# Per-head roots as one power on GpSimd, and rotary products, sums of squares and norm remainders on VectorE

## The chip, the cores and the metric

The kernel runs on one core of one Trainium2 chip. The metric is the device time of one execution in microseconds; the median of three runs of the kernel before is 3424.99 us (3420.28 to 3428.63). TensorE does the matrix products, VectorE and GpSimd elementwise work, ScalarE activations and copies, and SyncE (SP) issues the DMAs. Each engine works through its own instructions in order; semaphores make one wait for another.

## The reference

The reference computes two layers over 1024 latent tokens and 256 context tokens of width 1024. Each layer normalises the tokens (RMS), scales and shifts them by a modulation vector, projects them once, and hands the columns of that projection to latent attention (six heads), a state space part (S5) and windowed attention (six query heads, two key heads). An output projection and a gated feed-forward follow. The change lies in the preparation of queries and keys:

```python
def rms_norm(x, g):
    xf = x.astype(F32)
    y = xf * lax.rsqrt(jnp.mean(xf * xf, axis=-1, keepdims=True) + NORM_EPS)
    return (y * g.astype(F32)).astype(x.dtype)

def mla_queries(c_q, g_lora, w_uq, g_qk, rope):
    q = (rms_norm(c_q, g_lora) @ w_uq).reshape(b, t, MLA_HEADS, MLA_QK)
    q = rms_norm(q, g_qk)
    if rope is not None:
        q = jnp.concatenate([q[..., :MLA_NOPE], apply_rope(q[..., MLA_NOPE:], rope)], axis=-1)

def swa_queries(q_raw, g_qk, rope):
    q = rms_norm(q_raw.reshape(b, t, SWA_HEADS, SWA_HEAD_DIM), g_qk)
    return apply_rope(q, rope) if rope is not None else q
```

So each head of each token needs one reciprocal root of a mean of squares, and its (partial) rotation. Root and rotation commute, because the root is one factor for the whole head.

## The kernel before, in words

Tokens are taken 128 at a time on the partitions. The chunks are 512, 512 and 256 tokens (the last is the context). Every 32-bit product is made of three matmuls of rounded parts: `hi` (rounded on ScalarE) and `lo` (the remainder, made on VectorE), `mm3`. TensorE thus needs both parts of each operand.

The input projection of a layer (lines 522 to 840) works in four kinds of steps, each on a pair of token tiles, 256 tokens. `s1_pair` makes windowed keys and values and the shared rotary part of the latent keys, five pairs. `lora` makes 512-token feature chunks of `c_kv` or `c_q` (`chi`, `clo`, and the squares `csq`, summed over features). `s3` makes latent keys and values from `c_kv`, five pairs; `s5q` latent queries from `c_q`; `s7` windowed queries. The last two have five pairs in layer 0 and four in layer 1, where the context needs no queries. In each step TensorE fills PSUM tiles `tk` (four buffers). ScalarE copies them out to `kb`, `qb` or `sqb` (one tag, three buffers) and squares them into `sq`. VectorE sums the squares (`ssq_of`), takes the reciprocal root (`rsqrt`, eleven instructions), and multiplies by it (`mulr`). GpSimd rotates (`rope`, four products and sums; for context tokens one product with the gain). DMAs on SP write the result to DRAM (`kd`, `qd`, `sqd`, `skd`), from where attention reads it.

`norm_stats` sums the squares of the residual stream and `norm_apply` normalises and splits it. GpSimd takes some of their instructions: the sums for k = 3 and 5, and, with `eng=G`, the remainders for odd k, which need an extra copy on ScalarE. `norm_stats` already takes its root as one power on GpSimd (`rsqrt_pool`, line 180; `rn` in the trace).

The order of the work on each engine is set when the program is built: the source gives priorities, and instructions whose inputs come late let others pass, so that pieces of neighbouring steps are mixed. At run time an engine does not leave that order. Attention follows, mixed with the S5 part, whose tables GpSimd computes in long series.

The lines that the steps of the prediction touch: 170 (`rsqrt`), 273 and 297 (the norms), 568 and 579 (`rope_table`, `rope`), 602 (`rinv`), 620 (`s1_pair`), 643 (`lora`), 668, 705 and 732 (`s3`, `s5q`, `s7`). Many instructions carry the line of a helper, so the tile names tell them apart: L80 is `tt`, L93 and L95 are `ts`, L98 is `stt`, L77 `act`, L65 `mm`.

Of the kernel before, what the change touches and what calls it, by code (L numbers as in the profile page):

```python
# [8 lines left out]
F32 = mybir.dt.float32  # L9
# [23 lines left out]
def trunk(ctx, tc, x, c, ctxt, c_ctx, w_mod, b_mod, norm1, w_in, q_lora_g, w_uq, kv_lora_g, w_ukv,  # L33
# [24 lines left out]
    mhalf = const.tile([128, 4], F32, name="mhalf")  # L58
# [45 lines left out]
    def load_split(hi, lo, raw, srcs, scale=None):  # L104
        """DRAM pieces into raw, then hi = the rounded value and lo = what is left of it."""
        for dst, src in srcs:
            nc.sync.dma_start(out=dst, in_=src)
        if scale is None:
            act(hi, raw)
            sub(lo, raw, f32(hi))  # L110
        else:
            act(hi, raw, AF.Copy, scale=scale)
            stt(lo, raw, scale, f32(hi), ALU.mult, ALU.subtract)

    class Wsets:
        """Rotating sets of (rounded, rest, raw) weight tiles over the pools that are open."""
# [31 lines left out]
    class Side:  # L148
        """A generator of pieces of work, run up to a share of its steps."""
# [20 lines left out]
    def rsqrt(pl, dst, v, shape, tag):  # L170
        i = pl.tile(shape, I32, tag=tag + "i", name="rsi")
        w = pl.tile(shape, F32, tag=tag + "w", name="rsw")
        ts(i, v.bitcast(I32), 1, op0=ALU.logical_shift_right)
        ts(dst.bitcast(I32), i, -1, 0x5F3759DF)
        for _ in range(3):
            stt(w, v, -0.5, dst, ALU.mult, ALU.mult)
            mul(w, w, dst)
            stt(dst, w, 1.5, dst, ALU.add, ALU.mult)

    def rsqrt_pool(dst, v, n):  # L180
        """v to the power of -1/2, in one instruction of the general engine."""
        tt(dst, v, mhalf[:, 0:n], ALU.pow, G)
# [58 lines left out]
    def mod_cols(psf, pl, acc, l, nm, k0, n, nj):  # L241
        """Sums over the partitions of acc, n blocks of 128 columns for each of nj."""
# [13 lines left out]
    def mod_gen(l, nm, nj, pl, psf, w):  # L256
        """One modulation vector, with the sums over the rows on the vector engine."""
# [15 lines left out]
    def norm_stats(big, sm, psf, xs, ci, rn, o=0, n=None, eng=None):  # L273
        """rn[p, i] = 1 / rms of token i * 128 + p of the chunk (or of n of its tokens from o)."""
# [3 lines left out]
        for k in range(8):  # L278
# [3 lines left out]
            else:  # L282
                sq = big[1][:, z * 512:z * 512 + n] if big[1].shape[1] > 512 else big[1][:, 0:n]
                act(sq, xs[k][:, t0:t0 + n], AF.Square)
                add(ss[z], ss[z], sq, (eng or (G if k < 6 else V)) if z else V)
# [11 lines left out]
    def norm_apply(tb, rbt, psf, rn, xs, at, A, sh, ci, o=0, n=None, eng=G):  # L297
        """at = x * rn * A + sh, split; tb and rbt are scratch."""
# [8 lines left out]
        for k in range(8):  # L307
# [4 lines left out]
            if k % 2 and eng is G:  # L312
                act(t, t, AF.Identity, bias=sh[:, k, j:j + 1])
                sub(lo, t, f32(hi), G)
            else:
                stt(lo, t, sh[:, k, j:j + 1], f32(hi), ALU.add, ALU.subtract)
# [6 lines left out]
    def load_mov(cols, src, k0, m):  # L323
        """Columns of rows k0.. as a moving operand: m tiles of 128 rows in one set."""
# [27 lines left out]
    def s1_tiles(t0, m):  # L352
        """Tiles of tokens side by side, as the rows of the operands arrive."""
# [57 lines left out]
    def prep_x(ci, eng=None):  # L411
        t0, n = CHUNKS[ci]
        st = norm_stats(big, pp, fps, xs, ci, rn[:, ci], eng=eng)
# [27 lines left out]
    def params(rows, name):  # L441
        """Vectors of both layers, rows of 128 values each, with the channel on the partitions."""
# [26 lines left out]
    run(prep_x(0, V))  # L469
# [18 lines left out]
    a0 = norm_apply(tb0, rb0, sps, rn[:, 0], xs, at, modt[0]["A1"], modt[0]["h1"], 0, eng=V)  # L488
# [26 lines left out]
    for l in range(2):  # L515
# [6 lines left out]
        # ======== input projection ========  # L522
# [45 lines left out]
        def rope_table(g, half):  # L568
            """Cosines and sines of the latent tokens, times the gains of the dimensions they meet."""
# [4 lines left out]
            for o, s in ((0, 0), (half, half), (w, half), (w + half, 0)):  # L574
                mul(tab[:, :, o:o + half], tab[:, :, o:o + half],
                    g[:, :, s:s + half].to_broadcast([128, NL, half]), G)
            return tab

        def rope(xv, tab, g, t, nh, half, eng=None):
            """Gain and rotation of [128, 2, nh, 2 half] in place, two tiles of tokens."""  # L580
            eng = eng or G
            w = 2 * half
            sh = [128, 2, nh, w]
            if t >= NL:
                mul(xv, xv, g.unsqueeze(1).to_broadcast(sh), eng)
# [5 lines left out]
            mul(t1, xv, tb[:, :, :, 0:w].to_broadcast(sh), eng)  # L591
            for z in range(2):
                mul(t2[:, :, :, z * half:(z + 1) * half], xv[:, :, :, (1 - z) * half:(2 - z) * half],
                    tb[:, :, :, w + z * half:w + (z + 1) * half].to_broadcast([128, 2, nh, half]), eng)
            add(xv, t1, t2, eng)
# [6 lines left out]
        def rinv(ssq, nh):  # L602
            r = kp.tile([128, 2 * nh], F32, tag="rinv", name="rinv", bufs=2)
            rsqrt(kp, r, ssq, [128, 2 * nh], f"hn{nh}")
# [11 lines left out]
        # k_rope, windowed keys and values, with the token on the partitions  # L616
# [3 lines left out]
        def s1_pair(t0, part=None):  # L620
# [14 lines left out]
            ts(ssq, ssq, 1.0 / 64, EPS)  # L635
            rope(ks, tab_sk, gain["sgk"], t0, 2, 32)
            rope(krs[:, t0:t0 + 2, :].unsqueeze(2), tab_k, gain["gk"][:, :, 64:96], t0, 1, 16)
            mulr(ks, ks, rinv(ssq, 2), 2, 64)
# [4 lines left out]
        def lora(ws, g, ci, pre=()):  # L643
            n = CHUNKS[ci][1]
            cs, tot = [], None
            for f, w in enumerate(ws):
# [9 lines left out]
                else:  # L656
                    add(tot[:, :n], tot[:, :n], sq[:, :n], G)
# [9 lines left out]

        def s3(state):
            """Keys and values of the latent attention, from a chunk of c_kv."""
# [6 lines left out]
            rsqrt(kp, r[:, :nt], v[:, :nt], [128, nt], f"kv{nt}")  # L676
# [1400 lines left out]
```

## Time and profile before

| | before |
|---|---|
| runs, median (lowest to highest) | 3424.99 us (3420.28 to 3428.63) |
| profiled execution, span from first to last instruction | 3426.8 us; no time beside the span is given for it |
| TensorE busy, granted clock | 3253.7 us (95%), 0.971 |
| VectorE busy | 2339.9 us (68%), 4391 instructions |
| ScalarE busy | 1167.5 us (34%), 2076 instructions |
| GpSimd busy | 486.9 us (14%), 787 instructions |

Times in the profile are from one execution; 3426.8 us is 1.8 us above the median of the runs. The start of a row counts from the first instruction. A busy TensorE is not TensorE at its full rate: the granted clock tells at which of its levels it ran. A row's "idle before" is the time in which the engine had nothing to do just before, with the instruction that ended it.

### The profile page before, as it was taken

To read this page: it belongs to the slowest core of one execution; us is meant where nothing else is said; L and a number is where in the kernel's file an instruction comes from. 1 tells how busy PE (TensorE), PEld (TensorE's weight loads), DVE (VectorE), ACT (ScalarE), POOL (GpSimd) and SP (SyncE) were. 2 spreads that over 40 slices of the span, in tenths; PEclk is the share of its full clock that TensorE was granted. 3 is DMA by queue.
4 is the path that set the end of the run, shared out by engine and by line. 5 is a ranking of instruction groups with operands and counts; after the bars stand their busy time and mean duration, and the time that the engine had idled before them with its cause. 6 is when DMAs were issued, how large, how long until landed. Compare 5 with 4: busy or idle time off the path is not lost. (4 is left out here: it accounts for less than half of the span.)

```text
span 3426.8 us, 43150 instructions
## 1 busy us (share of the span) xinstructions
PE 3253.7 (95%) x15950; PEld 2597.1 (76%) x15950; DVE 2339.9 (68%) x4391; ACT 1167.5 (34%) x2076; POOL 486.9 (14%) x787
## 2 busy tenths in 40 slices
PE   8999769999999999999999999679999999999999
PEld 5897446667888888888888887446677788888888
DVE  7778786885687766667666768776762665555655
ACT  3532225555152222222223442234563422222221
POOL 2332561000020000000000432471000100000000
PEclk9999789999999999999999999789999999999999
DMA  7434111333512222222212344010324111111211
GB/s 247 132 87 125 32 50 41 98 116 100 166 47 77 64 73 73 64 65 78 62 59 68 101 117 116 18 31 23 87 71 124 44 44 49 56 43 43 62 37 56
DMA packets 401325, 260.84 MB, mean 76 GB/s; under 512 B 173647, under 2 KB 370393, under 8 KB 401113
## 3 DMA queue, kind: packets, MB, share of 16 engines
q1 hardware_dynamic: 400466, 257.80, 26.0%
q8 instruction: 126, 2.06, 0.2%
q14 instruction: 86, 0.70, 0.1%
q10 hardware_dynamic: 647, 0.26, 0.0%
HBM read 206.22 MB, written 49.46 MB: 75 GB/s over the span
## 5 line engine op out<-in xcount | busy, mean ns | idle before, releaser
L65 PE MATMUL u<-ah,wh 128*128 128x512 f32 (+1 forms) x1760 | 649.9, 370 | 2.3 <-ACT ah L77 1.6
L65 PE MATMUL u<-al,wh 128*128 128x512 f32 (+1 forms) x1760 | 648.9, 369 | 1.4 <-POOL al L80 1.1
L65 PE MATMUL u<-ah,wl 128*128 128x512 f32 (+1 forms) x1760 | 648.3, 368 | 0.0
L77 ACT ACTIVATE wh<-raw 128x1024 fp32r<-128x1024 f32 (+3 forms) x184 | 189.2, 1038 | 720.5 <-PE d L65 292.2
L98 DVE SCALAR_TENSOR_TENSOR cv<-u,par,cv 128x511 f32<-128x511 f32 (+2 forms) x616 | 326.1, 555 | 135.6 <-ACT cv L77 130.4
L65 PEld LDWEIGHTS u<-al,wh 128*128 128x128 f32 x1760 | 332.3, 189 | 58.2 <-POOL al L80 2.2
L65 PEld LDWEIGHTS u<-ah,wh 128*128 128x128 f32 x1760 | 332.0, 189 | 57.8 <-ACT ah L77 1.8
L65 PEld LDWEIGHTS u<-ah,wl 128*128 128x128 f32 x1760 | 332.2, 189 | 55.3
L80 DVE TENSOR_TENSOR wl<-raw,wh 128x1024 fp32r<-128x1024 f32 (+3 forms) x184 | 220.1, 1200 | 160.0 <-ACT wh L77 158.9
L98 DVE SCALAR_TENSOR_TENSOR x<-d,g,x 128x512 f32<-128x512 f32 (+2 forms) x307 | 209.5, 685 | 108.8 <-PE d L65 108.6
L98 DVE SCALAR_TENSOR_TENSOR macc<-mw,srow,macc 128x256 f32<-128x256 f32 (+1 forms) x364 | 231.3, 660 | 67.1 <-DMA mw<-in_w_mod_dram 65.8
L77 ACT ACTIVATE cv<-u,par,par 128x512 f32<-128x512 f32 (+1 forms) x220 | 159.7, 728 | 323.1 <-PE u L65 320.9
L65 PE MATMUL av<-p,v 128*65 128x512 f32 (+1 forms) x504 | 260.7, 601 | 0.0
L77 ACT ACTIVATE p<-s 128x512 f32<-128x512 f32 (+1 forms) x252 | 147.6, 586 | 236.4 <-PE s L65 233.1
L65 PE MATMUL d<-ah,wh 128*128 128x512 f32 (+2 forms) x614 | 224.8, 366 | 1.8 <-DVE x L98 1.6
L65 PE MATMUL d<-al,wh 128*128 128x512 f32 (+2 forms) x614 | 223.5, 364 | 0.0
L65 PE MATMUL d<-ah,wl 128*128 128x512 f32 (+2 forms) x614 | 223.4, 364 | 0.0
L1336 DVE TENSOR_REDUCE mx<-b 128x1 f32<-128x512 f32 (+1 forms) x300 | 165.6, 586 | 47.6 <-PE b L65 46.3
L65 PE MATMUL b<-kh,qh 96*128 96x512 f32 (+1 forms) x300 | 124.7, 462 | 63.0 <-DVE ql L98 46.0
L65 PE MATMUL s<-qh,kh 97*128 97x512 f32 (+1 forms) x252 | 154.0, 611 | 0.0
L65 PEld LDWEIGHTS b<-kh,qh 96*128 96x128 f32 x300 | 57.9, 199 | 114.5 <-DVE ql L98 50.8
L65 PE MATMUL av<-sp,sv 128*65 128x384 f32 x320 | 129.0, 492 | 6.5 <-ACT sden L77 3.4
(373 smaller groups left out, 6689.4 us busy)
## 6 DMA issues: line engine op xcount, KB each, us to landing
raw<-in_w_up_dram SPq DMA_DIRECT2D x88, 512.0 KB
mw<-in_w_mod_dram SPq DMA_DIRECT2D x224, 128.0 KB
raw<-in_w_down_dram SPq DMA_DIRECT2D x44, 512.0 KB
mw<-in_w_mod_dram SPq DMA_DIRECT2D x48, 256.0 KB
wm<-in_w_mod_dram SPq DMA_DIRECT2D x16, 512.0 KB
xd<-x SPq DMA_DIRECT2D x32, 256.0 KB
raw<-in_w_in_dram SPq DMA_DIRECT2D x14, 512.0 KB
sqd<-sqb SPq DMA_DIRECT2D x36, 192.0 KB
```

The costliest lines, as they stand in the source:

```text
L65: PE.matmul(out, lhsT, rhs, start=start, stop=stop)
L77: S.activation(out, in_, func, **kw)
L80: (eng or V).tensor_tensor(out, a, b, op=op)
L98: V.scalar_tensor_tensor(out, a, s, b, op0=op0, op1=op1)
L1336: V.tensor_reduce(mx[:, j, i:i + 1], ps[:, :w], axis=AX.X, op=ALU.max)
```

## The change

The eleven-instruction root `rsqrt` goes; all roots become one `pow` with -1/2 on GpSimd. The products of the rotations and of their tables, the sums of squares in `lora` and `norm_stats`, and the odd remainders of `norm_apply` move from GpSimd to VectorE. In `s5q`, `s7` and `s1_pair` the root is asked for before the rotation. In `s3`, `s5q` and `s7` the multiplication by the root, and the store, are put into a function that `scaling` runs when the next step has come to the same point. The diff also removes docstrings and comments, which are left out here.

```diff
-    mhalf = const.tile([128, 4], F32, name="mhalf")
+    mhalf = const.tile([128, 12], F32, name="mhalf")
...
-    def rsqrt(pl, dst, v, shape, tag):
-        i = pl.tile(shape, I32, tag=tag + "i", name="rsi")
-        w = pl.tile(shape, F32, tag=tag + "w", name="rsw")
-        ts(i, v.bitcast(I32), 1, op0=ALU.logical_shift_right)
-        ts(dst.bitcast(I32), i, -1, 0x5F3759DF)
-        for _ in range(3):
-            stt(w, v, -0.5, dst, ALU.mult, ALU.mult)
-            mul(w, w, dst)
-            stt(dst, w, 1.5, dst, ALU.add, ALU.mult)
...
     def rsqrt_pool(dst, v, n):
         tt(dst, v, mhalf[:, 0:n], ALU.pow, G)
...
-                add(ss[z], ss[z], sq, (eng or (G if k < 6 else V)) if z else V)
+                add(ss[z], ss[z], sq)
...
             act(hi, t, AF.Identity, bias=sh[:, k, j:j + 1])
-            if k % 2 and eng is G:
-                act(t, t, AF.Identity, bias=sh[:, k, j:j + 1])
-                sub(lo, t, f32(hi), G)
-            else:
-                stt(lo, t, sh[:, k, j:j + 1], f32(hi), ALU.add, ALU.subtract)
+            stt(lo, t, sh[:, k, j:j + 1], f32(hi), ALU.add, ALU.subtract)
...
                 mul(tab[:, :, o:o + half], tab[:, :, o:o + half],
-                    g[:, :, s:s + half].to_broadcast([128, NL, half]), G)
+                    g[:, :, s:s + half].to_broadcast([128, NL, half]))
...
-            mul(t1, xv, tb[:, :, :, 0:w].to_broadcast(sh), eng)
+            mul(t1, xv, tb[:, :, :, 0:w].to_broadcast(sh))
             for z in range(2):
                 mul(t2[:, :, :, z * half:(z + 1) * half], xv[:, :, :, (1 - z) * half:(2 - z) * half],
-                    tb[:, :, :, w + z * half:w + (z + 1) * half].to_broadcast([128, 2, nh, half]), eng)
-            add(xv, t1, t2, eng)
+                    tb[:, :, :, w + z * half:w + (z + 1) * half].to_broadcast([128, 2, nh, half]))
+            add(xv, t1, t2)
...
         def rinv(ssq, nh):
-            r = kp.tile([128, 2 * nh], F32, tag="rinv", name="rinv", bufs=2)
-            rsqrt(kp, r, ssq, [128, 2 * nh], f"hn{nh}")
+            r = kp.tile([128, 2 * nh], F32, tag="rinv", name="rinv", bufs=3)
+            rsqrt_pool(r, ssq, 2 * nh)
             return r
...
             ts(ssq, ssq, 1.0 / 64, EPS)
+            rr = rinv(ssq, 2)
             rope(ks, tab_sk, gain["sgk"], t0, 2, 32)
             rope(krs[:, t0:t0 + 2, :].unsqueeze(2), tab_k, gain["gk"][:, :, 64:96], t0, 1, 16)
-            mulr(ks, ks, rinv(ssq, 2), 2, 64)
+            mulr(ks, ks, rr, 2, 64)
...
-                    add(tot[:, :n], tot[:, :n], sq[:, :n], G)
+                    add(tot[:, :n], tot[:, :n], sq[:, :n])
...
+        waiting = []
+
+        def scaling(fn):
+            if waiting:
+                waiting.pop()()
+            if fn:
+                waiting.append(fn)
...
             ts(v[:, :nt], lora_stat(tot, ci), 1.0 / 256, EPS)
-            rsqrt(kp, r[:, :nt], v[:, :nt], [128, nt], f"kv{nt}")
+            rsqrt_pool(r[:, :nt], v[:, :nt], nt)
...
                 rr = rinv(ssq, 6)
-                mulr(kb[:, :, :, 0:64], kb[:, :, :, 0:64], rr, 6, 64)
-                mul(kb[:, :, :, 64:96], krs[:, t0:t0 + 2, :].unsqueeze(2).to_broadcast([128, 2, 6, 32]),
-                    rr.rearrange("p (a h) -> p a h", a=2).unsqueeze(3).to_broadcast([128, 2, 6, 32]), G)
                 for i in range(2):
                     nc.sync.dma_start(out=vd[:, t0 + i].rearrange("h p d -> p h d"), in_=vb[:, i])
-                    nc.sync.dma_start(out=kd[:, t0 + i].rearrange("h p d -> p h d"), in_=kb[:, i])
+
+                def scaled(kb=kb, rr=rr, t0=t0):
+                    mulr(kb[:, :, :, 0:64], kb[:, :, :, 0:64], rr, 6, 64)
+                    mul(kb[:, :, :, 64:96], krs[:, t0:t0 + 2, :].unsqueeze(2).to_broadcast([128, 2, 6, 32]),
+                        rr.rearrange("p (a h) -> p a h", a=2).unsqueeze(3).to_broadcast([128, 2, 6, 32]))
+                    for i in range(2):
+                        nc.sync.dma_start(out=kd[:, t0 + i].rearrange("h p d -> p h d"), in_=kb[:, i])
+                scaling(scaled)
...
-                rope(qb[:, :, :, 64:96], tab_q, gain["gq"][:, :, 64:96], t0, 6, 16)
                 ssq = ssq_of(sq, 6, 96)
...
-                mulr(qb, qb, rinv(ssq, 6), 6, 96)
-                for i in range(2):
-                    nc.sync.dma_start(out=qd[:, t0 + i].rearrange("h p d -> p h d"), in_=qb[:, i])
+                rr = rinv(ssq, 6)
+                rope(qb[:, :, :, 64:96], tab_q, gain["gq"][:, :, 64:96], t0, 6, 16)
+
+                def scaled(qb=qb, rr=rr, t0=t0):
+                    mulr(qb, qb, rr, 6, 96)
+                    for i in range(2):
+                        nc.sync.dma_start(out=qd[:, t0 + i].rearrange("h p d -> p h d"), in_=qb[:, i])
+                scaling(scaled)
...
         for t in range(0, ntq, 2):
             s7(t)
+        scaling(None)
         close_tkp()
```

`s7` is changed as `s5q` is, with the four stores to `sqd` in its `scaled`. The calls of `norm_stats`, `norm_apply`, `prep_x` and `apply` lose their `eng` argument.

## Rows read from the trace of the kernel before

**Rows 1.** The page's busy times: engine, us, share, instructions.
```profile
PE 3253.7 (95%) x15950; PEld 2597.1 (76%) x15950; DVE 2339.9 (68%) x4391; ACT 1167.5 (34%) x2076; POOL 486.9 (14%) x787
```

**Rows 2.** Busy time by stretch: length, engines in turn, clock, DMA share, GB/s.
```profile
60.00:290.00 230.00, 217.92 (x1275) 200.35 (x1274) 167.76 (x423) 97.40 (x255) 92.64 (x106) 0.97 0.44 120
290.00:520.00 230.00, 173.99 (x777) 111.03 (x776) 190.70 (x400) 69.14 (x141) 113.75 (x206) 0.83 0.24 62
1905.00:2100.00 195.00, 185.31 (x1056) 169.85 (x1056) 142.69 (x357) 80.65 (x206) 88.01 (x101) 0.98 0.42 104
2100.00:2320.00 220.00, 167.35 (x715) 106.94 (x715) 164.54 (x357) 67.61 (x133) 105.75 (x206) 0.82 0.18 45
```

**Rows 3.** TensorE's waits, 60 to 310 us: total us, times, longest.
```profile
PE tk L65 <- DVE clo L98: 3.5, 1, 3.5
PE sm L65 <- DVE rb L93: 2.7, 4, 1.3
PE tk L65 <- ACT vb L77: 1.9, 2, 1.2
```

**Rows 4.** TensorE's waits, 1890 to 2110 us.
```profile
PE tk L65 <- DVE wl L80: 3.0, 2, 2.2
PE f L65 <- ACT us L77: 2.5, 1, 2.5
PE tk L65 <- DVE clo L98: 1.6, 1, 1.6
PE tk L65 <- POOL al L80: 1.0, 1, 1.0
PE sm L65 <- POOL csq L80: 0.8, 1, 0.8
```

**Rows 5.** Timeline, one windowed pair, VectorE (DVE) and GpSimd (POOL): start us, us.
```profile
2065.62 0.96 DVE L80 TENSOR_TENSOR sqb<-sqb,rinv 128x768 f32<-128x768 f32 x1
...
2070.55 1.87 POOL L80 TENSOR_TENSOR sqb<-ra,rb 128x768 f32<-128x768 f32 x1
2070.74 1.71 DVE L80 TENSOR_TENSOR rsw<-rsw,rinv 128x12 f32<-128x12 f32 x1
...
2073.51 0.17 DVE L80 TENSOR_TENSOR rsw<-rsw,rinv 128x12 f32<-128x12 f32 x1
2073.72 0.17 DVE L98 SCALAR_TENSOR_TENSOR rinv<-rsw,rinv 128x12 f32<-128x12 f32 x1
2073.99 0.96 DVE L80 TENSOR_TENSOR sqb<-sqb,rinv 128x768 f32<-128x768 f32 x1
```

**Rows 6.** VectorE's groups by shape, 1905 to 2100 us: busy, mean ns | idle before.
```profile
L80 DVE TENSOR_TENSOR rsw<-rsw,rinv 128x12 f32<-128x12 f32 x39 | 12.3, 316 | 1.2
...
L599 DVE TENSOR_REDUCE ssq<-sq 128x12 f32<-128x1152 f32 x4 | 5.4, 1345 | 6.4 <-ACT sq L77 6.4
```

**Rows 7.** Timeline of four powers on GpSimd, and VectorE beside the last.
```profile
1873.09 0.70 POOL L80 TENSOR_TENSOR rn<-nv,mhalf 128x2 f32<-128x2 f32 x1
...
1890.39 1.03 POOL L80 TENSOR_TENSOR rn<-nv,mhalf 128x4 f32<-128x4 f32 x1
...
955.72 1.94 POOL L80 TENSOR_TENSOR rn<-nv,mhalf 128x4 f32<-128x4 f32 x1 [0.60 <-DVE nv L95]
...
1906.99 1.46 POOL L80 TENSOR_TENSOR rn<-nv,mhalf 128x4 f32<-128x4 f32 x1 [1.66 <-DVE nv L95]
1907.61 0.74 DVE L98 SCALAR_TENSOR_TENSOR al<-nb,h,ah 128x512 fp32r<-128x512 f32 x1
```

**Rows 8.** Busy time of two stretches of 20 us, columns as in rows 2.
```profile
220.00:240.00 20.00, 16.05 (x92) 15.58 (x91) 17.12 (x44) 8.04 (x21) 6.07 (x8) 0.83 0.37 99
...
2020.00:2040.00 20.00, 17.65 (x118) 17.13 (x117) 13.32 (x32) 9.13 (x24) 8.61 (x9) 0.87 0.23 63
```

**Rows 9.** Timeline in layer 0's attention, VectorE and TensorE.
```profile
480.12 22.46 DVE L98 SCALAR_TENSOR_TENSOR macc<-mw,srow,macc 128x512 f32<-128x512 f32 x2
503.29 0.58 PE L65 MATMUL b<-kh,qh 96*128 96x256 f32 x1 [20.97 <-DVE ql L98]
```

More of the change, by code (lines that the diff above doesn't have):

```diff
@@ L271, in mod_gen, with norm_stats @@
             yield
-    def norm_stats(big, sm, psf, xs, ci, rn, o=0, n=None, eng=None):
+    def norm_stats(big, sm, psf, xs, ci, rn, o=0, n=None):
         t0, n = CHUNKS[ci][0] + o, n or CHUNKS[ci][1]
@@ L295, in norm_stats, with norm_apply @@
         yield
-    def norm_apply(tb, rbt, psf, rn, xs, at, A, sh, ci, o=0, n=None, eng=G):
+    def norm_apply(tb, rbt, psf, rn, xs, at, A, sh, ci, o=0, n=None):
         t0, n = CHUNKS[ci][0] + o, n or CHUNKS[ci][1]
@@ L409, in trunk, with prep_x @@
     acc = [[xs[2 * z + q][:, 512:1024] for q in range(2)] for z in range(2)]
-    def prep_x(ci, eng=None):
+    def prep_x(ci):
         t0, n = CHUNKS[ci]
-        st = norm_stats(big, pp, fps, xs, ci, rn[:, ci], eng=eng)
+        st = norm_stats(big, pp, fps, xs, ci, rn[:, ci])
         for k in range(8):
@@ L467, in vec2 @@
         return v.rearrange("l (k p) -> (l k) p", p=128)
-    run(prep_x(0, V))
+    run(prep_x(0))
     use_wm(0)
@@ L487, in trunk @@
     tb0 = []
-    a0 = norm_apply(tb0, rb0, sps, rn[:, 0], xs, at, modt[0]["A1"], modt[0]["h1"], 0, eng=V)
+    a0 = norm_apply(tb0, rb0, sps, rn[:, 0], xs, at, modt[0]["A1"], modt[0]["h1"], 0)
     next(a0)
@@ L575, in rope_table, with rope @@
                 mul(tab[:, :, o:o + half], tab[:, :, o:o + half],
-                    g[:, :, s:s + half].to_broadcast([128, NL, half]), G)
+                    g[:, :, s:s + half].to_broadcast([128, NL, half]))
             return tab
-        def rope(xv, tab, g, t, nh, half, eng=None):
-            eng = eng or G
+        def rope(xv, tab, g, t, nh, half):
             w = 2 * half
@@ L584, in rope @@
             if t >= NL:
-                mul(xv, xv, g.unsqueeze(1).to_broadcast(sh), eng)
+                mul(xv, xv, g.unsqueeze(1).to_broadcast(sh))
                 return
@@ L739, in s7, with scaled @@
                 act(sq[:, i * 384:(i + 1) * 384], ps[:, 0:384], AF.Square)
-            rope(qb, tab_sq, gain["sgq"], t0, 6, 32)
             ssq = ssq_of(sq, 6, 64)
             ts(ssq, ssq, 1.0 / 64, EPS)
-            mulr(qb, qb, rinv(ssq, 6), 6, 64)
-            for i in range(2):
-                for z in range(2):
-                    nc.sync.dma_start(out=sqd[:, t0 + i, :, z, :].rearrange("h p d -> p h d"), in_=qb[:, i])
+            rr = rinv(ssq, 6)
+            rope(qb, tab_sq, gain["sgq"], t0, 6, 32)
+            def scaled():
+                mulr(qb, qb, rr, 6, 64)
+                for i in range(2):
+                    for z in range(2):
+                        nc.sync.dma_start(out=sqd[:, t0 + i, :, z, :].rearrange("h p d -> p h d"), in_=qb[:, i])
+            scaling(scaled)
         ntp, close_ntp = open_pool("ntp", side=sd)
@@ L757, in apply @@
         def apply(ci):
-            return norm_apply(tb, rbt, sbank, rn[:, ci], xs, at, mdv["A1"], mdv["h1"], ci, eng=G if l else V)
+            return norm_apply(tb, rbt, sbank, rn[:, ci], xs, at, mdv["A1"], mdv["h1"], ci)
         def save_x(ci):
@@ L1998, in rest @@
                     yield from norm_apply(tb, big[2][:, 1024:], nbank, rn[:, ci], xs, at, modt[1]["A1"],
-                                          modt[1]["h1"], ci, eng=V)
+                                          modt[1]["h1"], ci)
                 fill = Side(rest() if pi < 2 else st.g, 11)
```

## The prediction

> **What bounds the kernel now.** I read the page's busy times first, then busy time by stretches, then what TensorE waited for in the stretches that the change touches, then the timelines of VectorE and GpSimd there. TensorE is busy for 3253.7 of 3426.8 us [rows 1], so a change on other engines pays only where TensorE waits or where its clock falls. The stretches [rows 2] say where that is. The input projections (60 to 290 us in layer 0, 1905 to 2100 us in layer 1) hold 12.1 and 9.7 us without TensorE work, at a granted clock of 0.97 and 0.98. The first 220 to 230 us of attention behind each hold 56.0 and 52.7 us of it at 0.83 and 0.82: the larger part of the loss, but made of code that the diff does not edit.
>
> Inside the projections the waits are few. Layer 0: 3.5 us for the remainder `clo`, 2.7 for the broadcast `rb`, 1.9 for the copy `vb` [rows 3]. Layer 1: 3.0 for `wl`, 2.5 for `us`, 1.6 for `clo`, 1.0 for `al`, 0.8 for `csq` [rows 4]. After such a wait the clock is lower for a while: 220 to 240 us has a mean of 0.83 and 2020 to 2040 us one of 0.87 [rows 8], a mix of the levels 2.4 and 1.2 GHz. These are what there is to gain; most of them end on VectorE.
>
> VectorE is late there because of GpSimd. In one pair of windowed queries (rows 5), the root's product `rsw` takes 0.17 us when GpSimd is idle and 1.71 us when it starts just after GpSimd's 1.87 us sum, and ends with it. Over layer 1's projection the 39 `rsw` products average 316 ns [rows 6], against 0.17 us unblocked.
>
> **The change part by part.**
>
> Roots. Per layer there are five roots of width 4 for s1 and three for `kvr`, and fifteen (layer 0) or thirteen (layer 1) of width 12 from s3, s5q and s7: 44 in all, 11 VectorE instructions each, 484 go. From one start to the next in a chain is 0.21 us [rows 5], so a chain is 2.3 us unblocked, and 484 are 102 us; by the mean of the `rsw` group 3.9 us a chain. In their place stand 44 powers on GpSimd. The trace has powers of 2 columns (0.70 us) and of 4 (1.03, 1.46 and 1.94 us) [rows 7]. None is 12 wide: below, it takes at least the 1.03 us of 4 columns; above, three times 1.94, 5.8 us. I take 0.70 plus 10 columns at (1.03 - 0.70) / 2, 2.3 us, by the two undisturbed rows. The longer ones ran beside VectorE products of two inputs and seem to have waited for them. For the 12-wide ones even 5.8 us is hidden: `scaling` uses the root only after the next pair's rotation, GpSimd has little else left in the projection, and a windowed pair lasts 8.37 us (start to start of `sqb`, rows 5). In s1 the power runs under the key's rotation.
>
> Rotations and products. Unblocked product costs on VectorE go from 0.17 us at 12 columns to 0.96 at 768 [rows 5], 1.05 ns a column: 0.56 us at 384, 0.43 at 256, 0.36 at 192, 0.29 at 128. A rotation is four products: 3.0 us for s7, 1.8 for s5q, 1.4 + 0.8 for s1; s3 gets one of 0.56. With 8, 8 and 8 rotated pairs and 10 of s3 that is 24 + 15 + 18 + 6 us; with context gains, 32 table products and 16 sums of squares of the latents, about 88 us in both projections, and 5 us for norm work inside them: 93 added against 102 removed. Free of the lock, VectorE has about as much to do, in fewer and longer pieces. Its bounds are 93 us, unblocked, and 93 plus what the powers might hold it, below.
>
> Against TensorE's time per pair: s7 is 48 matmuls in 8.37 us, 0.174 us each; s3 is 24 such, 4.2 us; s5q is 36 of 288 instead of 384 columns, 4.7 us. VectorE per pair after: s7 reduction 0.9 (768 columns, by the 1345 ns of 1152 [rows 6]), rotation 3.0, scaling 0.96, 0.2 for a small one: 5.1 us of 8.37. s3: 0.9 + 0.4 for two small ones + 0.56 + 0.96, 2.8 of 4.2. s5q: 1.35 + 0.2 + 1.8 + 1.37 for scaling 1152 columns, 4.7 of 4.7, full but not over.
>
> What this takes from the waits. (a) `clo`, layer 0: ahead of it on VectorE stood a chain of 2.3 to 3.9 us, now a rotation of 1.8. I take 2.5 of the 3.5 us; it cannot give more than 3.5, or less than nothing. A mean clock of 0.83 is 6.8 us at the lower level in that 20 us stretch [rows 8]; less the wait itself some 3.3 us of matmuls at half speed, 1.6 us lost, of which 1.2 returns. (b) `rb` waits while GpSimd builds tables; those products are now VectorE's own, 0.29 to 0.43 each: 1.0 of 2.7, between 0 and 2.7. (c) `vb` stands for the wait on `kvr`: 2.3 us of chain against a power of 1.03 and its two handovers: I take 1.0 a wait, and 1.3 for the two waits, since one is shorter than that; if a `clo` product delays the power as in the 1.94 us row, 0.3. (d) Layer 1's `clo` and `csq`, 2.4, with (0.13 x 20 / 0.5 - 2.4) / 2 = 1.4 for the clock: 2.8 of 3.8. (e) `wl`, queued behind chain and reduction: 2.0 of 3.0. (f) `al` becomes one VectorE instruction of 0.74 us [rows 7] instead of a copy on ScalarE and a difference on GpSimd: 0.7 of 1.0. Sum: 2.5 + 1.2 + 1.0 + 1.3 + 2.8 + 2.0 + 0.7 = 11.5 us.
>
> The end of the projection, 2.5 us on `us`: I count nothing. The last pair's root falls from VectorE's path, but the pair before is scaled there too and its four stores stand in SP's queue ahead of the last four and of attention's loads; 2 us either way. In s5q the stores move the other way: deferred, they let the weight loads behind them on SP go first, already in (e). A deferred store keeps one of three `kb` buffers up to a pair longer, 4.7 us in s5q; the four PSUM tiles between ScalarE and TensorE, a quarter of that each, cover it.
>
> The norms outside the projections: 10 us of squares and 14 us of `al` go to VectorE, in stages where TensorE works on the output projection or the feed-forward. GpSimd's lock goes, VectorE's queue grows: I put 1 us against the change, between a gain of 2 and a loss of 4.
>
> In all 10.5 us less: 3426.8 - 10.5 = 3416.3 by the profiled span, which lies 1.8 us over the median of the runs; 3414.5 by the median. I forecast 3414 us.
>
> **A rule weighed.** In rows 7 a power runs from 1906.99 to 1908.45 us; a VectorE instruction with two inputs in SBUF (`al`) runs inside it in 0.74 us, near the 0.70 that the slope above gives for 512 columns. The Trainium skill, "SBUF — State Buffer", section "Who interferes with whom", says that such an instruction contends with a GpSimd instruction that reads SBUF, and that whichever began first has the port for its whole length. GpSimd's ordinary sum in rows 5 agrees; the power does not. By the rule alone the change would be slower, the first rival.
>
> **The rivals.**
>
> The power holds VectorE for its length. It strikes in s5q and s3, where each rotation or scaling would wait 2.3 us a pair: s5q 7.0 against 4.7, nine pairs, 21 us; s3 5.1 against 4.2, ten pairs, 9 us; s7 7.4 stays under 8.37. 30 us more: 3455, and at 5.8 us a power 52 + 44 and 23 in s7, 3544. It decides from 1.4 us a power in s3 and at once in s5q. Against it: rows 7. For it: no 12-wide power was seen. 5%.
>
> The waits are traded. The order on each engine is fixed beforehand, and a 1.8 or 3.0 us rotation in front of `clo` or `wl` holds them as the chain did. All of (a), (d) and (e) gone, 8.5 us less gain: 3423, with the end and the norms 3420 to 3431. For it: s5q fills VectorE. Against it: its total with the lock falls. 23%.
>
> Attention falls differently. TensorE's wait at 503.29 us is 20.97 us, because one VectorE sum, part of the 22.46 us row, starves beside back-to-back GpSimd work [rows 9]. Which VectorE instruction meets such a burst depends on when it comes. The two layers run the same code there and differ by 56.0 - 52.7 = 3.3 us; shifted by a few us, or ordered anew, a burst can swallow or release half of a 21 us wait. To 3403 and below 8%, to 3432 and above 7%.
>
> The roots do not come off the path: planned so that a scaling stands directly behind its power, VectorE waits 2.3 us as long as the chain lasted. 3425; 3%. Against it: `scaling` puts a rotation between.
>
> **How the numbers follow.** My forecast 3414, own range 3404 to 3421, has 54%; traded waits 23, attention 8 down and 7 up, the held port 5, roots on the path 3. About 0.2%, 6.9 us, is what a measurement of this kernel can tell from no change: faster means under 3418.1, slower over 3431.8. Faster: 50 of the 54 and the 8, 58%. Same: the remaining 4, 21 of the traded, the 3, 1 of attention: 29%. Slower: 13%. The range that leaves out 2 in 10 is 3396 to 3432.
>
> **What would show it.** Right: GpSimd in the projections holds little but powers of about 2.3 us; no VectorE product over its unblocked length there; `clo` and `wl` gone from TensorE's waits, the 20 us stretches after them at a clock near 1; attention's stretches still some 53 to 56 us short of TensorE work. Wrong: powers over 4 us or VectorE products stretched to a power's end; rotations standing before a late `clo`; or a difference that lies in attention and not in the projections.

## The result and the profile after

Four runs of the changed kernel took 3382.59 us in the median (3358.58 to 3383.88), four of the kernel before, beside them, 3426.2 us: ratio 0.9857, 95% interval 0.9826 to 0.9888. That is 43.6 us less where 10.5 us were forecast, and below the predicted range. The profiled execution took 3382.89 us. Its page of busy times, to be read against [rows 1] (PE is TensorE, PEld its weight loads, DVE VectorE, ACT ScalarE, POOL GpSimd):

```profile
PE 3233.7 (96%) x15950; PEld 2587.5 (77%) x15950; DVE 2275.3 (67%) x4143; ACT 1151.9 (34%) x2052; POOL 363.7 (11%) x595
```

TensorE is 20 us less busy with the same matmuls, which is clock (0.977 granted instead of 0.971), and idle some 26 us less. To see where, I divide both traces at events instead of times: an input projection lasts from the first to the last `tk` matmul, attention from there to the first `o` matmul, and the rest from there to the next projection or the last matmul. Lengths in us:

| kernel | start | projection 0 | attention 0 | rest 0 | projection 1 | attention 1 | rest 1 |
|---|---|---|---|---|---|---|---|
| before | 50.1 | 225.1 | 566.2 | 1040.0 | 201.0 | 513.3 | 825.7 |
| after | 49.0 | 217.4 | 545.5 | 1042.4 | 189.1 | 507.1 | 825.8 |
| difference | -1.1 | -7.7 | -20.7 | +2.4 | -11.9 | -6.2 | +0.1 |

The two projections gain 19.6 us, attention 26.9. Busy time by stretch of the kernel before, divided at these events (columns as in [rows 2]), the projections alone:

```profile
50.11:275.24 225.13, 213.05 (x1254) 197.23 (x1252) 166.88 (x414) 101.15 (x260) 89.69 (x103) 0.96 0.45 125
...
1881.39:2082.39 201.00, 190.81 (x1089) 174.86 (x1089) 151.82 (x373) 90.25 (x228) 85.29 (x98) 0.97 0.41 106
```

The same of the kernel after, each projection followed by the first 230 and 221 us of its attention:

```profile
49.02:266.40 217.38, 209.56 (x1254) 196.05 (x1252) 135.66 (x274) 101.55 (x260) 45.77 (x24) 0.97 0.47 130
...
266.40:496.00 229.60, 184.64 (x883) 122.78 (x882) 187.04 (x420) 74.33 (x152) 122.92 (x209) 0.88 0.28 72
...
1854.37:2043.44 189.07, 187.12 (x1089) 173.75 (x1089) 124.40 (x249) 88.10 (x224) 44.61 (x22) 0.98 0.45 114
...
2043.44:2264.00 220.56, 167.56 (x748) 110.67 (x748) 171.35 (x366) 66.55 (x130) 108.17 (x209) 0.86 0.22 52
```

Subtract TensorE's busy time from the length: the projections go from 12.1 and 10.2 us without TensorE work to 7.8 and 1.9, and TensorE's busy time in them falls by 3.5 and 3.7 us. VectorE sheds 31 and 27 us there. In these first parts of attention 45.0 and 53.0 us without TensorE work are left; the same first 230 and 221 us of the kernel before (from 275.24 and 2082.39 us) have 56.0 and 51.1. So layer 0 gains there, and layer 1 does not.

Over the whole of attention 0, TensorE's idle time falls by 10.8 us and its busy time by 9.9, which is clock. Of the 6.2 us of attention 1, 2.5 are the `us` wait at the end of the projection, which falls into attention by this division, and 3.1 are busy time. The three longest waits of attention 1 stay: 16.95, 9.54 and 13.86 us before, 16.89, 9.55 and 13.87 after.

What TensorE still waits for in projection 0 and projection 1 of the kernel after (against [rows 3, 4]):

```profile
PE sm L65 <- DVE rb L93: 2.2, 3, 1.0
PE tk L65 <- ACT vs L77: 2.0, 1, 2.0
PE sm L65 <- DVE csq L80: 1.5, 1, 1.5
PE tk L65 <- ACT vb L77: 1.1, 1, 1.1
...
PE tk L65 <- DVE clo L98: 1.2, 1, 1.2
PE tk L65 <- DVE wl L80: 0.3, 1, 0.3
```

A windowed pair of the kernel after, timeline of VectorE and GpSimd, answers [rows 5]:

```profile
2022.56 0.55 DVE L80 TENSOR_TENSOR rb<-sqb,tab 128x384 f32<-128x384 f32 x1
2022.79 2.44 POOL L80 TENSOR_TENSOR rinv<-ssq,mhalf 128x12 f32<-128x12 f32 x1 [3.82 <-DVE ssq L95]
2023.14 0.96 DVE L80 TENSOR_TENSOR sqb<-ra,rb 128x768 f32<-128x768 f32 x1
2025.27 0.96 DVE L80 TENSOR_TENSOR sqb<-sqb,rinv 128x768 f32<-128x768 f32 x1 [1.17 <-POOL rinv L80]
...
1942.86 2.35 DVE L80 TENSOR_TENSOR wl<-raw,wh 128x1024 fp32r<-128x1024 f32 x2
1943.09 4.25 POOL L80 TENSOR_TENSOR rinv<-ssq,mhalf 128x12 f32<-128x12 f32 x1 [0.80 <-DVE ssq L95]
```

The reader is to see four things. The power takes 2.44 us here, near the 2.3 estimated. A rotation sum runs inside it in 0.96 us, its unblocked length, while in [rows 5] the root's product was stretched to the end of a GpSimd sum. And the lock works the other way round: beside two `wl` remainders, of normal length, the power is 4.25 us. Last, the scaling waits 1.17 us for its own power: it does not stand behind the next pair's rotation.

In attention 0, the kernel before had two waits of TensorE of about 20 us, each behind a `macc` sum (products summed for the modulation) that VectorE could not finish, and one of 7.25 us behind a product `t` that took 9.31 us instead of 0.82. The first two are the one of [rows 9], and this, in its timeline of VectorE, TensorE and GpSimd:

```profile
360.76 19.23 DVE L98 SCALAR_TENSOR_TENSOR macc<-mw,srow,macc 128x512 f32<-128x512 f32 x1
...
362.20 1.41 POOL L80 TENSOR_TENSOR E<-cm,cm 128x256 f32<-128x256 f32 x2
...
375.01 3.21 POOL L80 TENSOR_TENSOR cm<-pq,bb 128x512 f32<-128x512 f32 x3
378.18 1.26 POOL L80 TENSOR_TENSOR q<-cm,cm 128x512 f32<-128x512 f32 x1
...
380.74 1.09 PE L74 MATMUL b<-ident,q 128*128 128x128 f32 x4 [18.05 <-DVE mx L1336]
```

A sum of 0.74 us takes 19.23: 21 products of the state space part follow each other on GpSimd without a gap, at their full rate, and the sum ends 0.55 us after the last of them. In the kernel after the later wait is left, and of the earlier one 9.81 us (timeline of VectorE and TensorE; the `macc` row holds two sums, of 21.62 and 0.74 us):

```profile
379.02 0.58 PE L65 MATMUL b<-kh,qh 96*128 96x256 f32 x1 [9.81 <-DVE ql L98]
...
451.08 22.29 DVE L98 SCALAR_TENSOR_TENSOR macc<-mw,srow,macc 128x512 f32<-128x512 f32 x2
474.08 0.58 PE L65 MATMUL b<-kh,qh 96*128 96x256 f32 x1 [20.83 <-DVE ql L98]
```

At the earlier place the two engines now take turns: from 363.18 us on three `t` products of 0.82 us take 5.71, and a GpSimd product of 1.33 us takes 1.92.

The Trainium skill, "SBUF — State Buffer", section "Who interferes with whom", says that a VectorE instruction with two SBUF inputs contends with a GpSimd instruction that reads SBUF. These rows agree, and show more: the loser waited for 21 instructions, not one. For the power the rule does not hold here in VectorE's direction (0.96 us inside the power).

### The profile page after: what moved, and what is told of

It reads as the page before. It is cut to its first block, busy times and chain, and to the rows that moved or that the text cites. A ratio compares the mean times of both kernels' runs of the same rounds, so it can differ in the third digit from the quotient of the medians.

```text
span 3381.1 us, 42563 instructions
## 1 busy us (share of the span) xinstructions
PE 3233.7 (96%) x15950; PEld 2587.5 (77%) x15950; DVE 2275.3 (67%) x4143; ACT 1151.9 (34%) x2052; POOL 363.7 (11%) x595
## 4 chain that ended last, share of the span: by engine, by line
PE 82%; DVE 11%; DMA 3%; ACT 2%; issue 1%; SPq 0%; POOL 0%; ACTq 0%; DVEq 0%; POOLq 0%
PE u L65 32%; PE d L65 11%; PE av L65 6%; PE tk L65 6%; PE o L65 5%; PE dx L65 5%; PE f L65 5%; PE b L65 5%; PE s L65 4%; PE b L74 2%; DVE macc L98 1%; DVE t L80 1%; DVE mx L1344 1%; DVE cpx L1057 1%; DVE sv L1164 1%
## 5 line engine op out<-in xcount | busy, mean ns | idle before, releaser
L98 DVE SCALAR_TENSOR_TENSOR macc<-mw,srow,macc 128x256 f32<-128x256 f32 (+1 forms) x364 | 212.0, 606 | 68.1 <-DMA mw<-in_w_mod_dram 66.9
L80 POOL TENSOR_TENSOR rn<-nv,mhalf 128x4 f32<-128x4 f32 (+1 forms) x11 | 13.7, 1241 | 1651.7 <-DVE nv L95 1651.7
```

The source lines that it names most:

```text
L80: (eng or V).tensor_tensor(out, a, b, op=op)
L98: V.scalar_tensor_tensor(out, a, s, b, op0=op0, op1=op1)
```

## The experiments

Two questions: which part of the change carries the projections, and what attention's gain has to do with the change. First the parts alone.

**Roots alone**: the kernel before, with `rinv` and `kvr` as powers.

```diff
...
-            rsqrt(kp, r, ssq, [128, 2 * nh], f"hn{nh}")
+            rsqrt_pool(r, ssq, 2 * nh)
...
```

> The kernel before with the roots alone as powers on GpSimd; rotations and products stay on GpSimd, nothing is deferred. Stages by TensorE: projection 0 from the first to the last tk matmul (before 225.2 us, after 217.4), projection 1 likewise (201.0, 189.0), attention 0 and 1 from there to the first o matmul (566.2 and 513.3; after 545.5 and 507.1). Theory 'chain' (the eleven small instructions, each of which GpSimd can hold, made VectorE late): both projections shrink by as much as in the changed kernel, 7 to 12 us each. Rival 'lock' (it is the rotations on GpSimd that hold VectorE, whatever it runs): they shrink by less than 4 us each, since the rotations are still there and each root now also queues behind one. On attention the theory 'meeting' (which VectorE instruction meets a long GpSimd series there depends on order and time) says attention 0 is anything from 540 to 570 us, with no relation to what the projection gained.

Measured: 3436.35 us (3400.70 to 3439.65, 10 runs), ratio 1.0011 (0.9985 to 1.0037): nothing gained. The ten runs lie in three groups: 3400.7, 3418.6 to 3420.1, and 3435.9 to 3439.7. Projection 0 is 232.7 us, 7.6 longer than before, projection 1 198.2, 2.8 shorter. What VectorE waited for in projection 0 of this kernel shows why:

```profile
DVE sqb L80 <- POOL rinv L80: 16.4, 3, 6.1
DVE qb L80 <- POOL rinv L80: 15.6, 5, 3.3
...
DVE kb L80 <- POOL rinv L80: 12.0, 5, 2.5
```

The powers stand on the engine that still has the rotations, and VectorE waits 44 us for them.

**Moves alone**: the kernel before, chains kept; rotations, tables, the latents' sums and the `s3` product on VectorE.

```diff
...
-            eng = eng or G
+            eng = eng or V
...
-                    add(tot[:, :n], tot[:, :n], sq[:, :n], G)
+                    add(tot[:, :n], tot[:, :n], sq[:, :n])
...
```

> The kernel before with the rotations, their tables, the sums of squares of lora and the one product of s3 on VectorE; the roots stay chains of eleven instructions on VectorE, nothing is deferred, the norms are as before. Theory 'lock': the projections shrink by most of what the change gave (5 to 10 us each), since nothing on GpSimd holds VectorE any more. Theory 'chain': VectorE now has 2.3 us of chain and the rotation in each pair, 7.0 us in s5q against TensorE's 4.7, so the projections get longer than before, by up to 20 us in layer 0 and 15 in layer 1; whole time 3420 to 3455.

Measured: 3374.74 us (3366.76 to 3389.99), ratio 0.9862 (0.9830 to 0.9893), projections 216.7 and 192.1 us. In the projections the moves alone give 17.3 of the 19.6 us. The whole times don't part the two kernels, since the runs of either spread over more than 20 us.

**Scaling at once**: the kernel after, with `scaling` running its function directly.

```diff
-            if waiting:
-                waiting.pop()()
             if fn:
-                waiting.append(fn)
+                fn()
```

> The changed kernel with scaling running its function at once instead of one step later. Theory that the deferral matters (roots hidden under the next pair's rotation): projections 2 to 10 us longer than the changed kernel's 217.4 and 189.0. Rival: the order planned for the engines already puts the scaling late, whatever the source says (VectorE's planned order differs in one instruction only): projections within 1 us of the changed kernel's, whole time 3383, or 3359 as in one of its runs.

Measured: 3381.15 us (3363.97 to 3382.92), ratio 0.9878 (0.9856 to 0.9900), as after; projections 216.3 and 187.2, 1.1 and 1.9 us shorter, so the theory falls; the rival's 1 us is missed on the other side. The planner had put each scaling right behind its power anyway: the order on TensorE, ScalarE and GpSimd is the same as in the kernel after, and VectorE's differs in one place.

**Norms back**: the kernel after, with the norms' odd squares and remainders on GpSimd again.

```diff
...
-                add(ss[z], ss[z], sq)
+                add(ss[z], ss[z], sq, (eng or (G if k < 6 else V)) if z else V)
...
```

> The changed kernel with the norms' GpSimd work back (sums for k = 3 and 5, remainders for odd k). If moving the norms cost time where TensorE runs the output projection and feed-forward: that stage of layer 0 (from the first o matmul to the first tk matmul of layer 1: before 1039.9 us, after 1042.5) goes back by 2 to 3 us. If it gained in the projection of layer 1 (al on VectorE): projection 1 grows by 1 to 3 us from 189.0. VectorE's planned order in attention 0 is the changed kernel's, so 'meeting' by order alone says attention 0 stays at 545 us; by time it may move. Whole time 3376 to 3392.

Measured: 3374.82 us (3364.76 to 3383.35), ratio 0.9855 (0.9823 to 0.9888); rest 0 1041.1 us instead of 1042.4; projections 214.9 and 191.0. The whole time can't be told from after. Projection 1 can: it is 1.9 us longer, as expected if `al` on VectorE gained there, and the waits on norm work are back in it (`al` 1.1 us, `nb` 1.2, `x` 0.9).

In the first four of these profiles attention 0 was 551.8, 530.6, 526.2 and 546.8 us, in steps that fit no part of the change: the wait of about 21 us near its 210th us was there in the first and the last, and missing in the other two. So the second set takes the suspected cause away.

**State space products on VectorE**, in three kernels: `phases` alone, and `phases` with `tables`, in the kernel after; both in the kernel before.

```diff
-                         "pm", G)
+                         "pm")
...
-                mul(t1, pr, cr, G)
+                mul(t1, pr, cr)
...
-                cmul(q[0], q[1], pr, pi, br, bi, sh, "pm", G)
+                cmul(q[0], q[1], pr, pi, br, bi, sh, "pm")
```

> The changed kernel with the state space part's `phases` products (192 a layer, 0.39 us each on GpSimd, 66 us a layer) on VectorE; its `tables` products stay on GpSimd. Theory 'starved': TensorE's 10 to 21 us waits in attention are VectorE instructions held by GpSimd's unbroken series of products; the longest series left is that of the tables, 12.3 us (365.83 to 378.18 us in the trace of before). So no VectorE instruction is held over 13 us, no wait of TensorE in attention over 14 us, and attention of layer 0 takes 526 us or less (545.5 in the changed kernel, 526.2 in its twin that scales at once), whole time 3355 to 3370. Rival 'room': VectorE has no room for some 30 us more a layer there; attention of layer 0 is 546 us or more, of layer 1 507 or more, whole time 3385 or more.

> The changed kernel with both `phases` and `tables` of the state space part on VectorE; GpSimd has next to nothing left in attention. Theory 'starved': no VectorE instruction over 3 us, all of TensorE's waits of 9 to 21 us in attention gone, in both layers; attention of layer 0 515 to 530 us, of layer 1 480 to 495 (507 in the changed kernel), whole time 3335 to 3355. Rival 'room': some 65 us more of VectorE work a layer stand in front of what TensorE waits for; attention is longer than in the changed kernel, 3390 or more.

> The kernel before, with its chains and with the rotations on GpSimd, but with `phases` and `tables` of the state space part on VectorE. Theory 'starved': what the change gained in attention has nothing to do with the instructions that it moves; the same comes without them. Input projections as before (225 and 201 us), attention of layer 0 515 to 535 us (566 before), of layer 1 480 to 500 (513 before), whole time 3355 to 3380. Rival 'order': attention gains because VectorE comes out of the projection with less queued; then attention of layer 0 stays at 555 or more, and the whole time at 3415 or more.

Measured: `phases` alone 3328.68 us (3323.73 to 3339.06), ratio 0.9720 (0.9702 to 0.9739); both, in the kernel after, **3311.12 us** (3309.38 to 3313.53), 0.9668 (0.9651 to 0.9684); both, in the kernel before, 3338.27 us (3335.28 to 3341.93), 0.9745 (0.9730 to 0.9760). Attention 0 and 1 are 527.8 and 467.7 us, 515.9 and 462.4, and 518.9 and 470.7. 'Starved' wins and 'room' and 'order' fall. The whole times are below its numbers in all three, and attention 0 fits them but for 527.8 with `phases` alone, where it had 526 or less. The second version beats both kernels by far, and the third takes 87.7 us off the kernel before (3425.93 beside it) without one instruction of the change. What it takes off are the starved waits: those over 6 us of the kernel before sum to 46.3 us in attention 0 and 40.3 in attention 1, and the two stages are 47.3 and 42.6 us shorter. That GpSimd's products were slow is not what TensorE waited for: waits that end on one of them are 0.5 us in the two stages of the kernel before together. TensorE's longest waits in the first 230 us of attention 0, of the kernel before and then of the third:

```profile
PE b L65 <- DVE ql L98: 28.8, 3, 21.0
PE b L74 <- DVE mx L1336: 18.1, 1, 18.1
...
PE b L65 <- DVE Sg L80: 6.7, 4, 3.2
PE b L65 <- DVE mx L1336: 5.0, 4, 2.6
```

and the third's busy times by stretch there, against [rows 2]:

```profile
274.88:505.00 230.12, 213.91 (x993) 143.00 (x993) 206.41 (x654) 89.81 (x185) 4.80 (x17) 0.94 0.30 77
2037.54:2258.00 220.46, 199.62 (x901) 130.92 (x901) 185.76 (x606) 85.03 (x171) 8.12 (x20) 0.94 0.25 58
```

These are 16.2 and 20.8 us without TensorE work, against the 56.0 and 51.1 named above. In all of attention 0 VectorE is busy 438.8 us with 240 instructions more, against 441.1 before: a starved instruction counts as busy, and that was as much as the products that moved. With `phases` alone two `t` are held, 4.90 us in attention 0 and 5.78 in attention 1, and no wait of TensorE is over 6.73.

**The changed kernel once more**, for its spread, no edit.

> The changed kernel once more, for its spread: its four runs were 3358.6 and 3382.3 to 3383.9, and its twin that scales at once, with the same order on every compute engine, had 3364.0 to 3382.9 and a profile of 3362 in which the 20.8 us wait of TensorE at 474 us was missing. Theory 'starved': runs fall into two heaps some 20 us apart, 3358 to 3365 and 3380 to 3384, and the profile shows the 20 us wait if it is of the upper heap, and not if it is of the lower. Rival: one heap, and a wait of 20 us in the profile whatever its time.

Measured: 3369.17 us, from 3360.04, 3361.80, 3376.53 and 3379.86; ratio 0.9836 (0.9809 to 0.9863). Attention 0 of the profile is 525.2 us, not 545.5. The order on every engine is the same, so the `macc` sum held at 451.08 us can be found again. GpSimd's row of products beside it in the kernel after, then both rows in this run (timelines of GpSimd and VectorE):

```profile
450.38 1.47 POOL L80 TENSOR_TENSOR cm<-E,s 128x128 f32<-128x128 f32 x4
...
449.20 2.69 POOL L80 TENSOR_TENSOR cm<-E,s 128x128 f32<-128x128 f32 x4
449.88 1.39 DVE L98 SCALAR_TENSOR_TENSOR macc<-mw,srow,macc 128x512 f32<-128x512 f32 x2
```

The sum begins 0.70 us after GpSimd's row in one run and 0.68 us after it in the other. In the first it is held for 21.62 us; here it passes in its normal time, and GpSimd's products are held instead (2.69 us for 1.47). Some 14 us later three more sums and the same series take turns (timeline of VectorE, TensorE):

```profile
464.04 5.30 DVE L98 SCALAR_TENSOR_TENSOR macc<-mw,srow,macc 128x512 f32<-128x512 f32 x3
...
469.78 0.50 PE L65 MATMUL b<-kh,qh 96*128 96x256 f32 x2 [2.23 <-DVE ql L98]
```

So the eight runs of the changed kernel lie in two heaps, 3358.6 to 3361.8 and 3376.5 to 3383.9: two profiles, one of each, differ by this wait.

**GpSimd's series later by time alone**: the kernel before, one product done two or four times (`range(3)` in the second); nothing else moves in any engine's order.

```diff
                 mul(t1, pr, cr, G)
+                if l == 0 and k == 0:
+                    for _ in range(1):
+                        mul(t1, pr, cr, G)
```

> The kernel before with one product (1.33 us) of GpSimd's first table series in layer 0 done twice: the order on every engine stays that of before, GpSimd's series comes 1.3 us later, and there is more work. Theory 'meeting by time': whether a VectorE instruction starves beside a series depends on when it comes; the wait of 18 us at 380 us or the one of 21 us at 503 us goes or another comes, and time and attention of layer 0 jump by 10 to 25 us, to 3400 to 3416 or to 3437 or more, here or in the next kernel. Rival 'order': the changed kernel lost the wait at 380 us because 71 instructions of VectorE stand elsewhere in attention; with the order of before both waits stay, 3423 to 3430.

> The same with three products more, GpSimd's series some 4 us later. Theory 'meeting by time': a jump of 10 to 25 us against the kernel before, as above. Rival 'order': both waits stay, 3425 to 3432.

Measured: 3420.45 us (3416.18 to 3425.92, 10 runs), ratio 0.9987 (0.9978 to 0.9996), and 3429.43 us (3424.79 to 3434.69, 10 runs), 1.0015 (1.0006 to 1.0024). No jump: the held sums stay, as in the timeline of the first one's VectorE,

```profile
359.00 18.61 DVE L98 SCALAR_TENSOR_TENSOR macc<-mw,srow,macc 128x512 f32<-128x512 f32 x1
...
471.40 22.50 DVE L98 SCALAR_TENSOR_TENSOR macc<-mw,srow,macc 128x512 f32<-128x512 f32 x2
```

The waits stay as 'order' said; the first of the two times lies some 2.5 us below its range. But the edit did not shift the meeting as it was meant to, because the VectorE sum came later or earlier together with the series. GpSimd's row of four `cm` products in which the first held sum begins is 0.85 us ahead of that sum in the kernel before (359.91 and 360.76 us), 1.47 in the first (357.53 and 359.00) and 0.65 in the second (363.35 and 364.00); at the second held sum the distance moves by less than 0.1 us. So 'meeting by time' is tested only for a series that comes 0.6 us earlier against the sum, and one 0.2 us later; and the changed kernel run again has shown both outcomes in one order. Attention 0 of the first is 558.3 us, 8 less than before with the same waits: that is TensorE's busy time (494.1 instead of 501.7), its clock. The order of VectorE in attention 0 does differ between before and after, in some 30 places, and TensorE's in as many. That this is what freed the sum at 380 us was not shown.

**Moves alone and roots alone, without starvation**: the second and first experiments, with the state space products on VectorE.

> The kernel before with the rotations, table products, sums of squares of the latents and the s3 product on VectorE, the roots still chains, norms and scaling as before, and the state space part's products on VectorE, so that attention holds no starved instruction. Theory 'lock': the moves alone carry the change; the input projections are 214 to 217 and 188 to 193 us, as in the changed kernel (216.1 and 189.0 there with the same attention), whole time 3307 to 3318 against 3311. Rival 'chain': without the powers VectorE has both the chains and the rotations, 195 us in the two projections; they stay within 5 us of 225 and 201, whole time 3325 to 3340.

> The kernel before with only the roots as powers on GpSimd, rotations still there too, and the state space part's products on VectorE. Theory 'lock': the powers queue behind GpSimd's rotations; no gain in the projections (226 to 234 and 197 to 202 us), whole time 3335 to 3347 against 3338. Rival 'chain': the chains were what held TensorE; projections 4 to 8 us shorter each, whole time 3320 to 3332.

Measured: 3316.43 us (3315.71 to 3317.86), ratio 0.9684 (0.9669 to 0.9698), projections 217.4 and 192.1; and 3349.07 us (3346.50 to 3355.27), 0.9785 (0.9768 to 0.9801), projections 233.3 and 199.7. On this quiet ground runs spread little, and the parts can be read off the medians: moves -21.8 us (3338.3 to 3316.4), roots alone +10.8 (projection 0 7.6 longer, projection 1 2.1 shorter), roots with deferral and norms on top of the moves -5.3, all together -27.2. With the moves alone the chains' groups, by shape, in projection 1 are

```profile
L98 DVE SCALAR_TENSOR_TENSOR rsw<-ssq,rinv 128x12 f32<-128x12 f32 x36 | 6.1, 171 | 0.9
L80 DVE TENSOR_TENSOR rsw<-rsw,rinv 128x12 f32<-128x12 f32 x36 | 6.1, 170 | 0.9
```

170 ns where [rows 6] have 316. The kernel with the same state space part but the rotations on GpSimd (the third above) has 328 for the second of these.

## Why the prediction was wrong

**The step that failed** is the one about attention: "the larger part of the loss, but made of code that the diff does not edit", entered at nothing, with 8% for a fall there. Attention lost 26.9 of the 45.7 us between the two profiles, 20.7 of them in layer 0, against 19.6 in the projections. The mechanism was in my own rows ([rows 9]) and in the third rival, which is what came true in layer 0: it fell differently which VectorE sum starves beside GpSimd's series, and for how long. In waits, the rival's price of half a 21 us wait was close, 10.8 us of idle time: the wait of 18.05 us became 9.81, and smaller ones moved. It left out the clock behind the waits, 9.9 us of busy time, and its chance was too small. In layer 1 nothing was released. The runs show how such a stage had to be treated: as long as both series and sums are there, attention 0 was anything from 525 to 567 us in these profiles, and one program shows values some 20 us apart. The range should have held a full wait on either side. That attention gained rather than lost is luck as far as the runs go, and so is the heap in which the median fell: the other one is some 20 us further below the forecast. Of the prediction's own signs of being wrong the last came by half: a difference that lies in attention, and in the projections too.

**The projections** were right in kind and sized too low, 19.6 us against 11.5. By terms, from the waits and stretches above:
- (a) `clo`, layer 0: 3.5 us gone, 1.0 back as a later `csq`: 2.5 in sum as said, though by another way.
- (b) `rb`: 0.5 instead of 1.0. (c) `vb` with `vs`: 3.2 before, 3.1 after, nothing instead of 1.3; a wait on `vs` took the place.
- (d) `clo` and `csq`, layer 1: 1.2 of the 1.4 counted as waits; `clo` keeps 1.2. (e) `wl`: 2.7 instead of 2.0. (f) `al`: 1.0 instead of 0.7.
- Not counted: waits of 0.3 to 1.0 us for norm and residual work beside the projections (`al` and `nb` in layer 0; `x`, `ntmp`, `nb`, `vb`, `vs` in layer 1), 2.0 and 3.4 us together, all gone or nearly. I had only looked at the top rows. With the norms back on GpSimd, projection 1 has 2.9 us more of waits on `al`, `nb` and `x` than the kernel after.
- The clock: TensorE's busy time fell by 3.5 and 3.7 us, where I put 1.2 and 1.4. After projection 1's waits the stretch of 0.87 [rows 8] has become one of 0.91 to 1.00. What each wait cost in clock the runs don't part; and the clock differs between profiles of the same order too: the first of the two shifted kernels, with the waits of before, has 3.3 us less busy time in projection 0 (209.8).
- The end: the `us` wait of 2.5 us, counted at nothing, is gone.

**GpSimd's lock** as the cause was right: the moves carry the gain, and a chain's product is 170 ns without the rotations beside it. But I gave both halves of the change one theory. The roots were not what held VectorE: alone they lose 10.8 us on quiet ground. VectorE waits for each power, and longest, up to 6.1 us, where the power and a rotation meet on GpSimd (`sqb`).

**VectorE's load**: 93 us added against 102 removed was too dark; VectorE's busy time in the projections fell by 58.6 us, since the stretched instructions went with the lock. The `s5q` pairs were not full: in layer 1 they follow each other in 6.4 to 8.3 us, not 4.7, and VectorE waits in them.

**The power** at 2.3 us was right (2.27 undisturbed, up to 4.25 beside `wl`). That "`scaling` uses the root only after the next pair's rotation" was wrong: VectorE waits 1.17 to 2.4 us a pair for the power, as the fourth rival had it. In projection 1 that costs TensorE little: what it still waits for is 1.8 us in all, for `clo`, `wl` and `x`, and nothing that a root scales.

**The norms** outside: rest 0 is 2.4 us longer, within the bounds of -2 to +4; I had taken 1. That it comes from the norms is not shown: kernels that leave the norms on GpSimd have 1040.0 to 1043.0 us there.

## What to carry to other kernels

Before costing an edit at the stage that it touches, look in the trace for single instructions many times longer than their twins; a VectorE sum of 0.74 us that takes 19 beside an unbroken GpSimd series is a loss to be taken away by itself. Here that was worth 87.7 us, three times the 27.2 that the change gives where nothing starves. While it was there, the length of its stage changed with the order and from run to run, and small edits can't be judged by the whole time; measure them on a version without it, and stage by stage. When work is split between two engines that hold each other up, move the work that blocks before the work that is blocked.

## What the runs showed of the hardware

- Where a VectorE sum with two inputs meets an unbroken series of two-input products on GpSimd, three things were seen. The sum passes and GpSimd's products are held (2.69 us for 1.47). The two take turns (three sums in 5.30 us). Or VectorE gets nothing until the series ends (21.62 us for a sum of 0.74). The first and the last came at the same place in two runs of one program, with the same order on all engines, the sum 0.70 and 0.68 us behind the start of GpSimd's row. What decides stays open.
- A copy is held too: `cpx`, 128 columns on 32 partitions, took 20.31 us beside such a series in attention 1 of the kernel before (at 2162.93 us), and 0.21 in the mean where the series are gone (both state space parts on VectorE).
- A power on GpSimd: 0.70 us for 2 columns, 1.01 for 4, 2.27 for 12. It didn't stretch the VectorE products that ran inside it (0.96 us for 768 columns) and was stretched by others, to 4.25 us.
- The state space products are shorter on VectorE: 0.23 us for a mean `cm` of `phases` against 0.37 on GpSimd, 0.68 against 1.20 for 512 columns, 0.82 against 1.37 for 640. GpSimd's means hold products slowed by turns; undisturbed ones took 1.10 and 1.33.
